# Order of low pieces, gate-up products and transposes in the expert stage of a retention-mLSTM block with expert-choice FFN

## Chip, cores and metric

The kernel runs on one core of one Trainium2 chip. The metric is the device time of one execution in microseconds (us); the median of several executions is compared. The engines are TensorE (PE, whose weight loads are shown apart as PEld), VectorE (DVE), ScalarE (ACT), GpSimd (POOL) and SyncE (SP, which here only issues loads).

## The reference, cut to what matters

One layer: `h = h + token_mixer(h)`, then `h = h + expert_choice_ffn(h)`, and a final norm. The change touches the second part. There are 528 tokens (16 of them meta tokens) of width 1024 and 16 experts; each expert takes the 66 tokens that score highest for it.

```
g, idx = lax.top_k(jnp.swapaxes(aff, 1, 2), cap)            # cap = 66
xs = jax.vmap(lambda ub, ib: ub[ib])(u, idx)                # [16, 66, 1024]
hid = (jax.nn.silu(jnp.einsum('becd,edf->becf', xs, w_gate))
       * jnp.einsum('becd,edf->becf', xs, w_up))            # [16, 66, 2816]
y = jnp.einsum('becf,efd->becd', hid, w_down) * g[..., None]
return jnp.zeros_like(h).at[jnp.arange(b_)[:, None, None], idx].add(y)
```

## The kernel before

All is float32 to the accuracy of three products: each operand is split into a high piece (rounded to fp32r by ACT, line 881) and a low piece (what is left, a subtraction on DVE, line 883), and each product is the sum of high x high (line 897), low input x high weight (898) and high input x low weight (899).

`experts` (line 840) runs 16 experts. Each has 48 slabs of weights, 128 x 1408 float32 (704 KB): gate half 0, up half 0, gate half 1, up half 1, with 8 slabs each (`wide`, 919), and down with 16 (`down`, 949; the last expert uses `last_down`, 963, with slabs of 1024 columns). `weights` (858) loads a slab through SP's queue into a ring of slabs. `product` (886) cuts a slab into two pieces of at most 768 columns, or into three of 512, 512 and 384 (the first slab of a projection, and some of down), splits each piece and issues the products on 66 rows. The pieces stand in two rings, six high and six low (three and three until the first expert's second half); that is three slabs.

Around the projections:

- `gate` (928): ACT writes the silu of the three gate banks into `hid` (line 931).
- `up` (933): DVE multiplies the three up banks into `hid` (line 937), in place.
- `hidden` (939): PE turns `hid` into 11 blocks of 128 x 66 (line 943, a transpose is a product with the identity), in two groups of 6 and 5; ACT and DVE split each group into `hT` (946, 947). It is called for half 0 after two slabs of gate half 1, and for half 1 after three slabs of down. Half 0 uses a `narrow` bank, half 1 a `wide` one.
- `gather` (902): POOL fetches the next expert's 66 rows by an indirect DMA (903), PE transposes them in two groups of four (910), DVE scales (915), ACT makes the high part of the input (916), POOL the low part (917).
- `scatter` (997): ACT weights the result (1000), POOL adds it to memory by an indirect DMA (1001).

The loop at line 1014 writes this order out. It is not the last word: the tile framework schedules each engine's instructions by a simulated timeline when the kernel is built, within the dependencies; each engine then executes its own list in order. `tc.issue_after(x)` adds an ordering edge: the instructions traced within it stand behind x on x's engine, with no semaphore. The generators (`wide`, `down`) yield after each slab, and `run(steps, n)` takes n slabs.

In names of the trace, left29t is the split input, right5t and left56t are the pieces, left24t is `hid` and left55t is `hT`; left25t to left48t are slabs.

Of the kernel before, what the change touches and what calls it, by code (L numbers as in the profile page):

```python
# [21 lines left out]
KT = 8  # L22
# [4 lines left out]
E = 16  # L27
CAP = 66
# [810 lines left out]
def experts(tc, a, bcast, left, right, routed, u_rows, h_rows, out):  # L839
# [5 lines left out]
    with ExitStack() as ctx:  # L845
# [31 lines left out]
        def split(src):  # L877
            n = src.shape[1]
            h = next(p_h)[:, :n]
            l = next(p_l)[:, :n]  # L880
            nc.scalar.activation(h, src, AF.Copy)  # L881
            with tc.issue_after(ready):
                nc.vector.tensor_sub(l, src, h)  # L883
            return h, l

        def product(slab, f0, cuts, target):
            n = slab.shape[1]
            for c0, c1 in zip((0,) + cuts, cuts + (n,)):
                h, l = split(slab[:, c0:c1])
                while c0 < c1:  # L890
# [8 lines left out]
                    nc.tensor.matmul(o, xh, l[:, w], start=False, stop=last)  # L899
                    c0 += m  # L900

        def gather(e):
# [4 lines left out]
            for g in range(2):  # L907
                b = bank()
                for j in range(4):
                    nc.tensor.transpose(b[:, j * CAP:(j + 1) * CAP], xg[:, 4 * g + j::KT], ident[:CAP, :CAP])  # L910
# [6 lines left out]
                (nc.gpsimd if e else nc.vector).tensor_sub(x_l[:, sl], v, x_h[:, sl])  # L917

# [9 lines left out]
        def gate(banks):  # L928
            for c, b in enumerate(banks):
                n = min(512, SLAB - 512 * c)  # L930
                nc.scalar.activation(hid[:CAP, 512 * c:512 * c + n], b[:CAP, :n], AF.Silu)

        def up(banks):
            for c, b in enumerate(banks):
                n = min(512, SLAB - 512 * c)
                s = slice(512 * c, 512 * c + n)
                nc.vector.tensor_mul(hid[:CAP, s], b[:CAP, :n], hid[:CAP, s])  # L937

        def hidden(hT, half):
            for f0, fn in ((0, 6), (6, 5)):  # L940
                b = bank("wide" if half else "narrow")
                for j in range(fn):
                    nc.tensor.transpose(b[:, j * CAP:(j + 1) * CAP], hid[:CAP, f0 + j:SLAB:RH], ident[:CAP, :CAP])  # L943
# [3 lines left out]
                nc.vector.tensor_sub(hT[:, 1, s], v, hT[:, 0, s])  # L947

# [61 lines left out]

        hT = None
        gather(0)
        nc.gpsimd.dma_start(tok, bass.AP(tensor=a["tok"].tensor, offset=a["tok"].offset, ap=[[0, CAP], [1, TOK]]))
        for e in range(E):
            g = wide(a["w_gate"], e, 0)
            gate(run(g))
            up(run(wide(a["w_up"], e, 0)))
            g = wide(a["w_gate"], e, 1)
            run(g, 2)
# [5 lines left out]
            hidden(hT, 0)  # L1025
            gate(run(g))
            up(run(wide(a["w_up"], e, 1)))
            if e == E - 1:
                break
            d = down(e, hT)  # L1030
            run(d, 3)
            hidden(hT, 1)
            gather(e + 1)
            scatter(e, run(d))
# [30 lines left out]
        d = last_down(E - 1, hT, 0)  # L1065
        run(d, 3)
        hidden(hT, 1)
        o = run(d)
# [73 lines left out]
```

## Time and profile before

| | us |
|---|---|
| median of 3 runs | 1989.85 (1989.01 to 1989.92) |
| profiled execution | 1988.62 |
| its span, first to last instruction | 1986.9 |
| granted clock of PE, mean over the span | 0.985 |

The expert stage runs from about 413 us to the end. Busy times are shares of the span. A row of a timeline has its start in us from the span's start, its length, engine, line and operation, output and inputs, the shapes, a count where rows are merged, and in brackets the idle time of the engine ahead of it with what ended that. Products overlap in the pipe, so the step from one start to the next, not the length, is what a product costs. A row of several instructions of one engine shows one length for all. A granted clock of 1.00 is 2.4 GHz, 0.50 is 1.2.

### The profile page before, as it was taken

How to read it: one execution, taken by the hardware profiler on the slowest of the kernel's cores; microseconds unless marked ns; L12 is line 12 of the kernel's file. 1: busy time of each engine (PE TensorE's matmuls, PEld its weight loads, DVE VectorE, ACT ScalarE, POOL GpSimd, SP SyncE). 2: the span in 40 equal slices, each digit the busy share in tenths (PEclk: the TensorE clock that was granted, in tenths of full speed). 3: DMA queues.
4: the chain of work that ended last, by engine and by line, in shares of the span. 5: the costliest groups of instructions: out<-in, count | busy, mean ns of one | idle time of the engine just before them, and what ended most of it. 6: DMA issues, size and time to landing. Idle time of an engine off the chain costs nothing.

```text
span 1986.9 us, 34790 instructions
## 1 busy us (share of the span) xinstructions
PE 1936.3 (97%) x12057; PEld 1513.4 (76%) x12057; DVE 1688.0 (85%) x2614; ACT 1450.9 (73%) x2417; POOL 307.4 (15%) x224
## 2 busy tenths in 40 slices
PE   8999999979999999999999999999999999999997
PEld 7989999767777777777777777777777777777674
DVE  7877776479999999898989888888888888888988
ACT  6565544277878888778777777787878787777776
POOL 1123221210000000030404010401030103030102
PEclk9999998989999999999999999999999999999999
DMA  4322214679999999999999999999999999999973
GB/s 156 98 77 76 65 56 169 233 283 361 373 362 378 352 392 350 363 368 360 376 357 377 352 370 352 382 354 363 360 363 365 353 366 362 371 367 368 344 280 115
DMA packets 134708, 604.60 MB, mean 304 GB/s; under 512 B 18597, under 2 KB 19237, under 8 KB 134531
## 3 DMA queue, kind: packets, MB, share of 16 engines
q1 hardware_dynamic: 123043, 565.28, 75.4%
q10 hardware_dynamic: 6656, 22.29, 3.3%
q0 software_dynamic: 4832, 14.82, 3.0%
q8 instruction: 94, 1.54, 0.3%
q14 instruction: 83, 0.68, 0.1%
HBM read 591.77 MB, written 10.55 MB: 303 GB/s over the span
## 4 chain that ended last, share of the span: by engine, by line
PE 90%; DVE 5%; DMA 2%; issue 1%; ACT 1%; POOL 0%; SPq 0%; POOLq 0%; DVEq 0%; ACTq 0%
PE wide L897 16%; PE wide L898 16%; PE wide L899 16%; PE narrow L899 8%; PE narrow L898 8%; PE narrow L897 8%; PE pj L210 2%; PE pj L211 2%; PE pj L212 2%; PE wide L943 1%; PE narrow L943 1%; DVE left24t L937 1%; PE pj L647 1%; PE pj L649 1%; PE pj L648 1%
## 5 line engine op out<-in xcount | busy, mean ns | idle before, releaser
L898 PE MATMUL wide<-right5t,left29t 128*66 128x512 f32 (+2 forms) x996 | 323.4, 329 | 0.5 <-DVE left29t L917 0.5
L897 PE MATMUL wide<-right5t,left29t 128*66 128x256 f32 (+2 forms) x996 | 316.7, 329 | 1.9 <-ACT left29t L916 1.6
L898 PE MATMUL wide<-left56t,left29t 128*66 128x256 f32 (+2 forms) x988 | 314.8, 326 | 0.0
L897 PE MATMUL wide<-left56t,left29t 128*66 128x256 f32 (+2 forms) x988 | 314.4, 327 | 0.0
L899 PE MATMUL wide<-right5t,left29t 128*66 128x512 f32 (+2 forms) x996 | 254.3, 330 | 0.3 <-DVE right5t L883 0.3
L899 PE MATMUL wide<-left56t,left29t 128*66 128x256 f32 (+2 forms) x988 | 245.4, 327 | 0.0
L897 PEld LDWEIGHTS wide<-left56t,left29t 128*66 128x66 f32 x988 | 135.0, 137 | 48.3 <-ACT left56t L881 1.7
L897 PEld LDWEIGHTS wide<-right5t,left29t 128*66 128x66 f32 x996 | 136.2, 137 | 43.0 <-ACT right5t L881 5.7
L899 PEld LDWEIGHTS wide<-right5t,left29t 128*66 128x66 f32 x996 | 134.6, 138 | 43.5 <-DVE right5t L883 0.7
L917 POOL TENSOR_TENSOR left29t<-right3t,left29t 128x264 fp32r<-128x264 f32 x30 | 155.7, 5206 | 70.6 <-ACT left29t L916 69.9
L899 PEld LDWEIGHTS wide<-left56t,left29t 128*66 128x66 f32 x988 | 132.3, 136 | 38.2
L903 POOL DMA_INDIRECT right3t<-u_rows,right3t x16 | 17.3, 1082 | 926.9 <-PE narrow L899 645.0
L898 PEld LDWEIGHTS wide<-left56t,left29t 128*66 128x66 f32 x988 | 134.5, 136 | 33.4
L898 PEld LDWEIGHTS wide<-right5t,left29t 128*66 128x66 f32 x996 | 136.1, 137 | 23.8 <-DVE left29t L917 0.9
L898 PE MATMUL narrow<-right5t,left55t 128*66 128x512 f32 x443 | 153.6, 352 | 0.0
L897 PE MATMUL narrow<-right5t,left55t 128*66 128x512 f32 x443 | 152.4, 352 | 0.0
L897 PE MATMUL narrow<-left56t,left55t 128*66 128x512 f32 (+1 forms) x441 | 151.4, 349 | 0.0
L210 PE MATMUL pj<-right1t,left2t 128*128 128x256 f32 (+1 forms) x496 | 144.5, 291 | 3.4 <-DVE left23t L387 3.4
L898 PE MATMUL narrow<-left56t,left55t 128*66 128x512 f32 (+1 forms) x441 | 147.6, 349 | 0.0
L211 PE MATMUL pj<-right2t,left2t 128*128 128x256 f32 (+1 forms) x496 | 143.6, 290 | 0.0
L212 PE MATMUL pj<-right1t,left3t 128*128 128x256 f32 (+1 forms) x496 | 143.2, 289 | 0.0
L899 PE MATMUL narrow<-right5t,left55t 128*66 128x512 f32 (+1 forms) x442 | 134.3, 355 | 0.7 <-DVE right5t L883 0.7
(497 smaller groups left out, 5057.6 us busy)
## 6 DMA issues: line engine op xcount, KB each, us to landing
left1t<-in_w_in_f ACTq DMA_DIRECT2D x30, 512.0 KB, 3.9
left43t<-in_w_up SPq DMA_DIRECT2D x12, 704.0 KB, 7.0
left42t<-in_w_up SPq DMA_DIRECT2D x12, 704.0 KB
left48t<-in_w_gate SPq DMA_DIRECT2D x12, 704.0 KB
left47t<-in_w_up SPq DMA_DIRECT2D x12, 704.0 KB, 6.3
left46t<-in_w_up SPq DMA_DIRECT2D x12, 704.0 KB
left25t<-in_w_up SPq DMA_DIRECT2D x12, 704.0 KB
left26t<-in_w_gate SPq DMA_DIRECT2D x12, 704.0 KB, 5.9
```

The source lines that it names most:

```text
L210: nc.tensor.matmul(ps[:, :ln], wh, x_h[:, k, l0:l0 + ln], start=(k == 0), stop=False)
L211: nc.tensor.matmul(ps[:, :ln], wh, x_l[:, k, l0:l0 + ln], start=False, stop=False)
L212: yield nc.tensor.matmul(ps[:, :ln], wl, x_h[:, k, l0:l0 + ln], start=False, stop=(k == KT - 1)).ins
L647: nc.tensor.matmul(ps[:, :ln], h, y_h[:, k, l0:l0 + ln], start=(j == 0), stop=False)
L648: nc.tensor.matmul(ps[:, :ln], h, y_l[:, k, l0:l0 + ln], start=False, stop=False)
L649: nc.tensor.matmul(ps[:, :ln], l, y_h[:, k, l0:l0 + ln], start=False, stop=(j == len(ks) - 1))
L897: nc.tensor.matmul(o, xh, h[:, w], start=start, stop=False)
L898: nc.tensor.matmul(o, xl, h[:, w], start=False, stop=False)
L899: nc.tensor.matmul(o, xh, l[:, w], start=False, stop=last)
L917: (nc.gpsimd if e else nc.vector).tensor_sub(x_l[:, sl], v, x_h[:, sl])
L937: nc.vector.tensor_mul(hid[:CAP, s], b[:CAP, :n], hid[:CAP, s])
L943: nc.tensor.transpose(b[:, j * CAP:(j + 1) * CAP], hid[:CAP, f0 + j:SLAB:RH], ident[:CAP, :CAP])
```

## The change

In each half of each expert the first slab of the next projection is traced ahead of `gate` and of `up`. In `up`, the first multiplication is put behind the last but one low piece traced so far, the other two behind the last one: these are the second and the third low piece of the next projection's first slab (in the last expert, whose down slabs have two pieces, the first and the second). `hidden` and `gather` become generators with one step per group of transposes. Each group of transposes is put behind the last product traced so far (`between`), and `paced` traces one slab behind each group. Half 0 starts after two slabs of gate half 1, half 1 after two of down (three before), and the gather's two groups follow those of half 1.

```diff
@@ split, product
-                nc.vector.tensor_sub(l, src, h)
+                lows.append(nc.vector.tensor_sub(l, src, h).ins)
             return h, l
+        latest = [None]
+        lows = []
...
-                    nc.tensor.matmul(o, xh, l[:, w], start=False, stop=last)
+                    latest[0] = nc.tensor.matmul(o, xh, l[:, w], start=False, stop=last).ins
                     c0 += m
+        def between():
+            return tc.issue_after(latest[0]) if latest[0] else nullcontext()
@@ gather (hidden in the same way)
-                for j in range(4):
-                    nc.tensor.transpose(b[:, j * CAP:(j + 1) * CAP], xg[:, 4 * g + j::KT], ident[:CAP, :CAP])
+                with between():
+                    for j in range(4):
+                        nc.tensor.transpose(b[:, j * CAP:(j + 1) * CAP], xg[:, 4 * g + j::KT], ident[:CAP, :CAP])
...
+                yield
@@ up
-                nc.vector.tensor_mul(hid[:CAP, s], b[:CAP, :n], hid[:CAP, s])
+                with tc.issue_after(lows[-1 if c else -2]):
+                    nc.vector.tensor_mul(hid[:CAP, s], b[:CAP, :n], hid[:CAP, s])
@@ the loop
+        def paced(steps, *others):
+            for x in others:
+                for _ in x:
+                    run(steps, 1)
+            return run(steps)
         hT = None
-        gather(0)
+        run(gather(0))
...
         for e in range(E):
-            g = wide(a["w_gate"], e, 0)
-            gate(run(g))
-            up(run(wide(a["w_up"], e, 0)))
+            g = run(wide(a["w_gate"], e, 0))
+            u = wide(a["w_up"], e, 0)
+            run(u, 1)
+            gate(g)
+            u = run(u)
             g = wide(a["w_gate"], e, 1)
-            run(g, 2)
+            run(g, 1)
+            up(u)
+            run(g, 1)
...
-            hidden(hT, 0)
-            gate(run(g))
-            up(run(wide(a["w_up"], e, 1)))
+            g = paced(g, hidden(hT, 0))
+            u = wide(a["w_up"], e, 1)
+            run(u, 1)
+            gate(g)
+            u = run(u)
+            d = last_down(E - 1, hT, 0) if e == E - 1 else down(e, hT)
+            run(d, 1)
+            up(u)
             if e == E - 1:
                 break
-            d = down(e, hT)
-            run(d, 3)
-            hidden(hT, 1)
-            gather(e + 1)
-            scatter(e, run(d))
+            run(d, 1)
+            scatter(e, paced(d, hidden(hT, 1), gather(e + 1)))
...
-        d = last_down(E - 1, hT, 0)
-        run(d, 3)
-        hidden(hT, 1)
-        o = run(d)
+        run(d, 1)
+        o = paced(d, hidden(hT, 1))
         d = last_down(E - 1, hT, 1)
```

## Rows read from the trace of the kernel before

**Rows 1.** The profile's page: the busy time of each engine in us with its share of the span and its instructions.

```profile
PE 1936.3 (97%) x12057; PEld 1513.4 (76%) x12057; DVE 1688.0 (85%) x2614; ACT 1450.9 (73%) x2417; POOL 307.4 (15%) x224
```

**Rows 2.** Busy time of each engine in two stretches of one expert each: start and end, length, then PE, PEld, DVE, ACT and POOL with their instructions, the granted clock, the DMA engines' busy share and GB/s.

```profile
591.50:686.90 95.40, 95.40 (x572) 71.71 (x571) 87.06 (x121) 78.93 (x122) 5.07 (x4) 1.00 0.99 369
971.00:1067.30 96.30, 96.03 (x572) 71.32 (x571) 84.98 (x121) 75.93 (x123) 21.59 (x5) 1.00 0.98 366
```

**Rows 3.** What SP's load queue waited for, the longest row: us in total, times, longest. left56t holds one part of the pieces, right5t the other.

```profile
SPq L866 <- DVE left56t L883: 613.2, 386, 14.2
```

**Rows 4.** Timeline of DVE around the multiplications of half 1 (line 937) in several experts. Between 965.55 and 966.76 stands one low piece of 512.

```profile
487.26 0.68 DVE L937 TENSOR_TENSOR left24t<-wide,left24t 66x512 f32<-66x512 f32 x1
...
772.74 0.83 DVE L883 TENSOR_TENSOR right5t<-left36t,right5t 128x640 fp32r<-128x640 f32 x1 [0.50 <-ACT right5t L881]
773.48 0.68 DVE L937 TENSOR_TENSOR left24t<-wide,left24t 66x512 f32<-66x512 f32 x1
...
869.18 0.69 DVE L937 TENSOR_TENSOR left24t<-wide,left24t 66x512 f32<-66x512 f32 x1 [1.84 <-PE wide L899]
...
965.55 0.69 DVE L937 TENSOR_TENSOR left24t<-wide,left24t 66x512 f32<-66x512 f32 x1 [1.85 <-PE wide L899]
966.76 1.15 DVE L937 TENSOR_TENSOR left24t<-wide,left24t 66x512 f32<-66x512 f32 x2
...
1158.22 0.69 DVE L937 TENSOR_TENSOR left24t<-wide,left24t 66x512 f32<-66x512 f32 x1 [1.85 <-PE wide L899]
...
1256.12 0.69 DVE L937 TENSOR_TENSOR left24t<-wide,left24t 66x512 f32<-66x512 f32 x1 [1.85 <-PE wide L899]
...
1935.25 1.75 DVE L937 TENSOR_TENSOR left24t<-wide,left24t 66x512 f32<-66x512 f32 x3 [0.53 <-PE wide L899]
```

**Rows 5.** Timeline of PE at the transposes of half 1 and of the gather in an early expert.

```profile
587.46 0.40 PE L898 MATMUL narrow<-left56t,left55t 128*66 128x512 f32 x1
587.69 1.44 PE L943 MATMUL wide<-right3t,left24t 66*128 66x66 f32 x11
588.96 0.27 PE L910 MATMUL wide<-right3t 66*128 66x66 f32 x1
589.04 0.54 PE L899 MATMUL narrow<-left56t,left55t 128*66 128x256 f32 x2
...
590.30 0.96 PE L910 MATMUL wide<-right3t 66*128 66x66 f32 x7
591.06 0.37 PE L897 MATMUL narrow<-right5t,left55t 128*66 128x384 f32 x1
```

**Rows 6.** The same for half 1 and the gather in a later expert.

```profile
1160.02 0.34 PE L898 MATMUL narrow<-right5t,left55t 128*66 128x384 f32 x1
1160.62 1.55 PE L943 MATMUL wide<-right3t,left24t 66*128 66x66 f32 x11 [0.27 <-DVE left24t L937]
1162.01 1.05 PE L910 MATMUL wide<-right3t 66*128 66x66 f32 x8
1162.87 0.46 PE L899 MATMUL narrow<-right5t,left55t 128*66 128x512 f32 x1
1163.13 0.62 PE L897 MATMUL narrow<-right5t,left55t 128*66 128x512 f32 x1
```

**Rows 7.** Stretches around the falls of the granted clock (PEclk), columns as in rows 2: ahead of the first fall within the expert stage's steady part, the first fall, and the last of four (the other two are at 1357 and 1552 us).

```profile
1159.70:1163.10 3.40, 3.13 (x24) 2.61 (x23) 3.40 (x6) 1.39 (x3) 0.00 (x0) 1.00 0.88 315
1163.10:1166.50 3.40, 3.40 (x13) 2.29 (x12) 3.40 (x8) 3.28 (x8) 3.06 (x2) 0.50 0.89 305
...
1842.40:1845.80 3.40, 3.40 (x13) 2.17 (x12) 3.40 (x7) 3.37 (x8) 2.24 (x1) 0.50 0.84 283
```

**Rows 8.** Timeline of ACT ahead of the mark at 965.55.

```profile
962.04 1.27 ACT L881 ACTIVATE right5t<-left47t 128x512 fp32r<-128x512 f32 x2 [0.39 <-PE wide L898]
```

**Rows 9.** Timeline of POOL in an early and in two later experts.

```profile
593.53 1.21 POOL L917 TENSOR_TENSOR left29t<-right3t,left29t 128x264 fp32r<-128x264 f32 x1 [0.58 <-ACT left29t L916]
...
875.38 19.15 POOL L917 TENSOR_TENSOR left29t<-right3t,left29t 128x264 fp32r<-128x264 f32 x2
...
1163.37 0.98 POOL L903 DMA_INDIRECT right3t<-u_rows,right3t  x1 [64.65 <-PE narrow L899]
```

**Rows 10.** Timeline of PE in the last expert: the transposes of half 1, and the waits in the tail.

```profile
1935.93 0.39 PE L898 MATMUL narrow<-right5t,left55t 128*66 128x512 f32 x1
1937.05 1.56 PE L943 MATMUL wide<-right3t,left24t 66*128 66x66 f32 x11 [0.73 <-DVE left24t L937]
...
1962.79 0.40 PE L898 MATMUL narrow<-left56t,left55t 128*66 128x512 f32 x1
1963.86 0.44 PE L899 MATMUL narrow<-right5t,left55t 128*66 128x512 f32 x1 [0.68 <-DVE right5t L883]
...
1968.47 0.45 PE L899 MATMUL narrow<-left56t,left55t 128*66 128x512 f32 x1 [0.69 <-DVE left56t L883]
```

**Rows 11.** Timeline of DVE behind the mark at 965.55.

```profile
968.89 0.81 DVE L883 TENSOR_TENSOR right5t<-left46t,right5t 128x640 fp32r<-128x640 f32 x1
969.62 0.95 DVE L883 TENSOR_TENSOR left56t<-left46t,left56t 128x768 fp32r<-128x768 f32 x1
```

**Rows 12.** Timeline of DVE around 890 us: a low piece of 384, and an idle time.

```profile
890.40 0.54 DVE L883 TENSOR_TENSOR right5t<-left25t,right5t 128x384 fp32r<-128x384 f32 x1
...
893.09 1.85 DVE L883 TENSOR_TENSOR right5t<-left26t,right5t 128x512 fp32r<-128x512 f32 x2 [0.35 <-ACT right5t L881]
```

More of the change, by code (lines that the diff above doesn't have):

```diff
@@ L1 @@
 import itertools
-from contextlib import ExitStack
+from contextlib import ExitStack, nullcontext
 import concourse.bass as bass
@@ L941, in hidden @@
                 b = bank("wide" if half else "narrow")
-                for j in range(fn):
-                    nc.tensor.transpose(b[:, j * CAP:(j + 1) * CAP], hid[:CAP, f0 + j:SLAB:RH], ident[:CAP, :CAP])
+                with between():
+                    for j in range(fn):
+                        nc.tensor.transpose(b[:, j * CAP:(j + 1) * CAP], hid[:CAP, f0 + j:SLAB:RH], ident[:CAP, :CAP])
                 v = b[:, :fn * CAP].rearrange("p (k c) -> p k c", c=CAP)
@@ L947, in hidden @@
                 nc.vector.tensor_sub(hT[:, 1, s], v, hT[:, 0, s])
+                yield
         def down(e, hT):
```

## The prediction

> **What bounds the kernel now.** I read the page first: TensorE (PE) is busy 97% of a span of 1986.9 us, VectorE (DVE) 85%, ScalarE (ACT) 73% [rows 1]. That alone says little, so next come the stretches of one expert each: PE is busy in 95.40 of 95.40 us in an early expert and in 96.03 of 96.30 us in a later one, with the DMA engines near 0.98 in both [rows 2]. The DMA share looks like a second bound. It is not one: the load queue waits 613.2 us for DVE to release slabs, on one part of the pieces alone [rows 3], so the loads run ahead and are held back. The expert stage is bound by PE, and only what makes PE wait or slows it can be won.
>
> The useful view is the period of the experts. The first multiplication of half 1 on DVE (line 937, first of three) reads the first bank that the up projection closes, so its start marks nearly the same place in every expert. I call it the mark. In the first experts the marks are at 487.26 and 773.48 us, three periods apart: 286.22 / 3 = 95.41 us. Then come 869.18 and 965.55 (96.37), 1158.22 and 1256.12 (97.90), and 1935.25 at the last expert [rows 4]. The same work thus has three periods, 95.41, 96.4 and 97.9, in one run.
>
> What differs is seen in two places. **Order on DVE.** In the early experts a low piece of the next projection's second slab (640 elements, line 883) already stands ahead of the mark and DVE hardly waits. In the later ones DVE sits idle for 1.85 us ahead of it, because the multiplications are queued in front of the first slab's low pieces [rows 4]. **Order on PE.** In the early form the 19 transposes behind half 1 stand as 12 and 7, products between, and the first follows its product of 512 columns after 0.23 us (587.46 to 587.69). In the later form they are one run, and PE goes from the product at 1160.02 to the transpose at 1160.62: 0.60 us where a product of 384 columns takes 0.23 x 384 / 512 = 0.17, so 0.43 us of waiting for DVE's multiplications [rows 5, 6]. In some periods the clock falls behind this run: granted 0.50 in the stretch from 1163.10 after one at 1.00, and so at four places, the last from 1842.40 [rows 7]. That is 1.2 GHz in place of 2.4.
>
> **The change part by part.**
>
> *Low pieces ahead of the multiplications.* At 32 places (two halves, 16 experts) the first multiplication goes behind two low pieces and the other two behind the third. No instruction is added. DVE's idle 1.85 us takes two pieces of 512 at 0.60 us (965.55 to 966.76 is one multiplication and one such piece) [rows 4], so they cost nothing, if their high pieces are there. ACT makes these, and its pieces of that slab (left47t) are done by 963.3, 2.2 us ahead of the mark [rows 8]. From the mark: first multiplication 0.60, third low piece 0.46 (0.54 less the 0.08 by which such rows overlap), the other two 1.07 (1.15 less 0.08), together 2.13 us. Now the later form takes 1.21 + 1.07 = 2.28 us [rows 4, 11, 12]. A small step earlier.
>
> *Transposes in groups.* In each half the first group waits for the last product of the second slab. A slab on PE takes (95.41 - 3.38) / 48 = 1.92 us, where 3.38 is the early transposes, 1.27 for each run of eleven, 0.08 and 0.76 [rows 5]. Two slabs are 3.83 us after the mark; the multiplications are done at 2.13. So the wait of PE for them, 0.43 us in each later expert, goes with 1.7 us to spare. It becomes no other wait that I can name: what is late next is the low pieces of the second slab (below). The transposes are as many as before. Six runs stand where the early form has three. The first product behind a run comes 0.26 after the one ahead of it rather than 0.23 (1162.87 to 1163.13, against 587.46 to 587.69) [rows 5, 6]: three more runs x 0.03 x 16 = 1.4 us. The ends: nothing, since seven transposes take 0.76 and eleven 1.27, no dearer each; and 0.12 a run, which is what a late run of eleven (1.39, 1160.62 to 1162.01) takes over an early one: 5.8 us. I take 1.4, nearest to the early rows.
>
> *Gather and hidden pieces as steps.* The gather's indirect DMA on POOL is traced one slab later, behind the two groups of hidden. It is issued at 1163.37, right behind the transposes of the gather before it (1162.01), and is wanted an expert later [rows 6, 9]; a step of 2 to 4 us is covered by some 90. The loads on SP keep their order; in the last expert one load of w_down now stands ahead of the four row loads, and SP's queue is held by slabs coming free anyway [rows 3]. The silu (ACT) is traced behind the first slab's high pieces; its result is used a projection (15 us) later. All of these: nothing, and if the slack were gone, one ACT step of 0.64 us (1.27 for two) per place [rows 8], inside the range's ends.
>
> *What the early order is worth.* The early experts already run with low pieces ahead and split transposes, without waits and at full clock. The change writes that order down for all. So I price it by the period: from 773.48 to 1935.25 are twelve periods, 1161.77 us, against 12 x 95.41 = 1144.92: 16.9 us [rows 4]. Of these the four falls of the clock are 4 x (97.90 - 96.37) = 6.1, the rest (10.8, 0.9 per expert) is the wait and the longer runs. Behind the last mark PE goes from 1935.93 to 1937.05, 1.12 where 0.23 is usual: 0.9 more [rows 10]. Sum: 16.9 + 0.9 - 1.4 = 16.4 us.
>
> Of the clock, [rows 7] show falls after a late run (0.43 us of waiting, 19 transposes); the early expert with the split form is at 1.00 throughout [rows 2]. The Trainium skill (TensorE: Matmul & The Clock Gate, "HAM oscillation") ties a falling clock to stretches in which PE sits idle. By that rule transposes are work, pacing them changes nothing about the falls, and the gain would be 10.3 us. The row speaks for the transposes: PE was busy 3.13 of 3.40 us ahead of the fall.
>
> **The sum.** The profiled execution took 1988.62 us, 1.72 outside its span; 1988.62 - 16.4 = 1972.2. The median of the runs is 1.23 above that execution: 1973.5 us, 0.8% faster. What measurement of this kernel can tell from no change is about 0.2%, 4 us.
>
> **The rivals.**
>
> 1. *The clock still falls.* Short runs of transposes may fall into the same stretch: against it, four early experts without one; for it, two groups of hidden and two of the gather come within 8 us. Four falls stay: 1973.5 + 6.1 = 1979.6.
>
> 2. *Low pieces of the second slab come late (slower).* After the mark DVE owes 2.13 us, then the second slab's pieces, 0.73 for 640 (968.89 to 969.62) and 0.87 for 768 (0.95 less 0.08) [rows 11]: 3.73 us. PE wants the last at about 3.83 - 0.29 = 3.54 (its product of 640 columns, 0.23 x 640 / 512), and the transposes that used to give DVE time now stand behind. Where PE has no high products to put in front, it waits, and the tail of the trace shows the price: 1.07 us from 1962.79 to 1963.86 where 0.23 is usual, so 0.84 us [rows 10]. Once at each of 32 places: 27 us, 1973.5 + 27 = 2000.4. It decides if the 0.2 us of lag is not covered. Against it: high products are put in front today (two products with high pieces stand ahead of the transposes of [rows 6], and the product with the low piece, line 899, comes behind), and there are pieces for three slabs.
>
> 3. *The gather's subtraction on POOL is locked out (slower).* One of its two instructions takes 1.21 us early, but both together 19.15 us later, ending where DVE sits idle for 0.35 us ahead of 893.09 [rows 9, 12]. The change fills DVE's idle time. If both groups waited 18 us, one after the other, from 10 us behind the mark, they would end 46 us behind it. The next projection starts at about 33 us (16 x 1.92 + 2.1 for transposes) and wants the second half of the low input four slabs later, at 41: 5 us x 15 = 75 us, 2048 us. The rule that says so is the Trainium skill's (SBUF — State Buffer, "SBUF: two separate sides"): DVE and GpSimd share ports under an exclusive lock, and the loser blocks; the rows agree. Against the price: DVE catches up sooner, since its 1.85 us are used, and the wait limits itself.
>
> 4. *The order does not change.* The pins might only restate what is scheduled in most places; then 1989.9. Against it: the late rows have the multiplications in front [rows 4].
>
> **How the numbers follow.** Forecast 0.78; rival 1, 0.08; rival 4, 0.05; rival 2, 0.06; rival 3, 0.03. Faster by over 0.2% is the forecast and rival 1: 0.86. Within: 0.05. Slower: 0.06 + 0.03 = 0.09. The range starts at 1989.9 - 17.8 (no cost for the runs) - 2.1, the three long waits of the tail (0.7 each, two of them shown) [rows 10] if DVE comes there with its lead, less 1 for the spread of runs: 1969. It ends at 1984: runs at 5.8 instead of 1.4 (1977.9) and the clock still falling (6.1).
>
> **What would show it.** Right: all marks some 95.4 to 95.5 us apart; low pieces ahead of each mark and no 1.85 us in front of it; no row of PE waiting on line 937; transposes in runs of 6, 5, 4, 4 with products between; a granted clock of 1.00 from 440 us to the tail. Wrong: waits of PE on line 883 outside the tail (rival 2), on the POOL subtraction (rival 3), half-rate stretches still there (rival 1), or periods of 96.4 still.

## The result, and the profile after

The changed kernel takes 1974.4 us (median, 1974.08 to 1977.21) beside 1989.43 us for the kernel before in the same runs: a ratio of 0.9929, 95% interval 0.9911 to 0.9946, so 0.7% faster. It ran a second time beside other kernels: 1976.22 against 1990.17, 0.9926, interval 0.9912 to 0.9939. The profiled execution took 1974.51 us with a span of 1972.8; the span of before was 1986.9. Forecast were 1973.5 us and a range of 1969 to 1984.

Line numbers moved with the edit: the products are lines 900 to 902 (897 to 899 before), the multiplications 947 (937), hidden's transposes 954 (943), the gather's 918 (910), its DMA 910 (903), its subtraction on POOL 925 (917), the silu 940. The pieces stay at 881 (high, ACT) and 883 (low, DVE).

The page first, against [rows 1]:

```profile
PE 1923.9 (98%) x12057; PEld 1511.5 (77%) x12057; DVE 1694.7 (86%) x2614; ACT 1455.4 (74%) x2417; POOL 177.6 (9%) x224
```

The instruction counts of PE and DVE are those of before. PE is busy 12.4 us less (1936.3 - 1923.9), out of 14.1 us of span. So most of what was won is PE doing the same instructions in less time, and some 1.7 us is idle time. The idle time understates the waits, though: of the 0.43 us that a step loses in [rows 6], the row has 0.27 as idle, and the rest counts as busy. POOL's busy time fell by 130 us, to which the last section comes back.

One early and one later expert, columns as in [rows 2]:

```profile
591.40:686.60 95.20, 95.20 (x572) 71.61 (x571) 87.22 (x121) 79.02 (x123) 4.80 (x4) 1.00 0.98 371
1064.00:1159.60 95.60, 95.60 (x572) 71.59 (x571) 85.82 (x121) 76.40 (x122) 3.93 (x4) 1.00 0.98 370
```

PE is busy in all of the later stretch too, at a granted clock of 1.00. In the whole expert stage of this trace, from 440 us to the tail, no stretch at 1.2 GHz is left; the next fall is at 1963.85, in the tail, where before had one as well.

The marks, on DVE, against [rows 4] (the first is early, the second the last one of the early form, the others late):

```profile
487.11 0.68 DVE L947 TENSOR_TENSOR left24t<-wide,left24t 66x512 f32<-66x512 f32 x1
...
772.85 0.68 DVE L947 TENSOR_TENSOR left24t<-wide,left24t 66x512 f32<-66x512 f32 x1
...
1057.72 0.69 DVE L883 TENSOR_TENSOR left56t<-left43t,left56t 128x512 fp32r<-128x512 f32 x1
1058.33 0.69 DVE L883 TENSOR_TENSOR right5t<-left43t,right5t 128x512 fp32r<-128x512 f32 x1
1059.66 0.69 DVE L947 TENSOR_TENSOR left24t<-wide,left24t 66x512 f32<-66x512 f32 x1 [0.65 <-PE wide L902]
1060.27 0.54 DVE L883 TENSOR_TENSOR right5t<-left43t,right5t 128x384 fp32r<-128x384 f32 x1
1060.73 1.14 DVE L947 TENSOR_TENSOR left24t<-wide,left24t 66x512 f32<-66x512 f32 x2
1061.80 0.81 DVE L883 TENSOR_TENSOR right5t<-left42t,right5t 128x640 fp32r<-128x640 f32 x1
...
1155.29 0.69 DVE L947 TENSOR_TENSOR left24t<-wide,left24t 66x512 f32<-66x512 f32 x1 [0.65 <-PE wide L902]
```

The order is the one the change writes down: two low pieces, the mark, the third low piece, the two other multiplications, the second slab. The multiplications end 2.14 us behind the mark, at the start of the next piece (1061.80 - 1059.66; forecast 2.13). DVE's idle time ahead of the mark went from 1.85 to 0.65, the 1.20 that two pieces of 512 take. The early period is (772.85 - 487.11) / 3 = 95.25 us, 0.16 less than before. The late one is 1155.29 - 1059.66 = 95.63, where before had 96.4 and, with a fall, 97.9.

PE at the same place, against [rows 6]:

```profile
1062.53 0.22 PE L901 MATMUL narrow<-right5t,left55t 128*66 128x128 f32 x1
1062.66 0.50 PE L902 MATMUL narrow<-right5t,left55t 128*66 128x128 f32 x2
...
1064.05 0.83 PE L954 MATMUL wide<-right3t,left24t 66*128 66x66 f32 x6
1064.69 0.31 PE L900 MATMUL narrow<-left56t,left55t 128*66 128x256 f32 x1
...
1066.63 0.77 PE L954 MATMUL wide<-right3t,left24t 66*128 66x66 f32 x5
...
1069.63 0.55 PE L918 MATMUL wide<-right3t 66*128 66x66 f32 x4
...
1071.96 0.55 PE L918 MATMUL wide<-right3t 66*128 66x66 f32 x4
```

Runs of 6, 5, 4 and 4, the first 4.39 us behind the mark, 2.25 us after the multiplications ended. No row of PE waits for line 947 in this trace. The only step at this place that is longer than a product is 1062.53 to 1062.66, 0.13 us where 128 columns take 0.06: the second slab's low piece of 640 (1061.80 on DVE, 0.81 long) is 0.07 us late.

**Where the 14.1 us came from.** The span divides at the marks: up to the fourth, 773.48 - 772.85 = 0.63; the twelve periods behind it, 1161.77 - (1920.65 - 772.85) = 13.97; the tail behind the last mark, 51.65 before and 52.15 after, -0.50. Sum 14.1.

One late period, taken apart by the steps of PE from one start to the next (each product at 0.23 us for 512 columns and in proportion, 91.08 us for 540 of them; what a step is longer than that counts as listed, and the last row holds all the excesses below 0.06 us):

| us in one late period | before (965.55) | after (1059.66) |
| --- | --- | --- |
| 540 products at their rate | 91.08 | 91.08 |
| 30 transposes | 3.62 | 3.08 |
| wait for the multiplications | 0.43 | 0 |
| wait for a low piece of the second slab | 0 | 0.07 |
| step at the scatter (first to second slab of the next gate) | 0.10 | 0.10 |
| small excesses | 1.10 | 1.30 |
| sum | 96.33 | 95.63 |

By this count the transposes gave more (0.54) than the wait (0.43 - 0.07 = 0.36), and the small excesses took 0.20 back. Apart from that, the twelve periods hold the four falls, 4 x 1.53 = 6.1 us.

### The profile page after: what moved, and what is told of

It reads as the page before. It is cut to its first block, busy times and chain, and to the rows that moved or that the text cites. A ratio compares the mean times of both kernels' runs of the same rounds, so it can differ in the third digit from the quotient of the medians.

```text
span 1972.8 us, 34817 instructions
## 1 busy us (share of the span) xinstructions
PE 1923.9 (98%) x12057; PEld 1511.5 (77%) x12057; DVE 1694.7 (86%) x2614; ACT 1455.4 (74%) x2417; POOL 177.6 (9%) x224
## 4 chain that ended last, share of the span: by engine, by line
PE 92%; DVE 4%; ACT 1%; DMA 1%; issue 1%; POOL 0%; POOLq 0%; SPq 0%; DVEq 0%; ACTq 0%
PE wide L900 16%; PE wide L902 16%; PE wide L901 16%; PE narrow L902 8%; PE narrow L901 8%; PE narrow L900 8%; PE pj L210 2%; PE pj L211 2%; PE pj L212 2%; PE wide L954 1%; PE narrow L954 1%; PE pj L647 1%; PE pj L649 1%; PE pj L648 1%; PE wide L918 1%
## 5 line engine op out<-in xcount | busy, mean ns | idle before, releaser
L900 PE MATMUL narrow<-left56t,left55t 128*66 128x512 f32 (+1 forms) x442 | 151.9, 347 | 0.0
L901 PE MATMUL narrow<-left56t,left55t 128*66 128x512 f32 (+1 forms) x442 | 146.1, 346 | 0.0
L902 PE MATMUL narrow<-left56t,left55t 128*66 128x512 f32 (+1 forms) x442 | 128.5, 346 | 1.8 <-DVE left56t L883 1.8
L210 PEld LDWEIGHTS pj<-right1t,left2t 128*128 128x128 f32 x496 | 96.2, 194 | 5.3 <-issue 2.9
```

What stands on the lines that cost most here:

```text
L210: nc.tensor.matmul(ps[:, :ln], wh, x_h[:, k, l0:l0 + ln], start=(k == 0), stop=False)
L900: nc.tensor.matmul(o, xh, h[:, w], start=start, stop=False)
L901: nc.tensor.matmul(o, xl, h[:, w], start=False, stop=False)
L902: latest[0] = nc.tensor.matmul(o, xh, l[:, w], start=False, stop=last).ins
```

## Experiments

All were timed in five rounds beside the kernel before. "Late period" is the distance of marks in the settled late experts of the profiled execution; "falls" are stretches at 1.2 GHz between 440 us and the tail.

| kernel | median us | ratio to before | late period | falls |
| --- | --- | --- | --- | --- |
| before | 1989.9 to 1990.5 | 1 | 96.37 (four of 97.9) | 4 |
| low pieces alone | 1989.93 | 1.0000 [0.9991, 1.0009] | 97.18 | 0 |
| pacing alone | 1999.50 | 1.0051 [1.0038, 1.0065] | 97.81 | 0 |
| changed, one run of transposes | 1976.50 | 0.9937 [0.9923, 0.9951] | 95.84 | 0 |
| low pieces alone, silu behind | 1977.67 | 0.9938 [0.9924, 0.9951] | 95.77 | 0 |
| before, gather apart | 1982.84 | 0.9962 [0.9949, 0.9976] | 96.37 | 0 |
| changed, silu in front | 2004.54 | 1.0068 [1.0054, 1.0082] | 98.4 (mean of nine) | 0 |
| changed, two slabs ahead | 1974.20 | 0.9927 [0.9914, 0.9941] | 95.47 | 0 |
| changed, scatter later | 1975.54 | 0.9926 [0.9912, 0.9939] | 95.63 | 0 |
| changed, both of these | 1976.71 | 0.9930 [0.9917, 0.9944] | 95.47 | 0 |
| changed, again | 1976.22 | 0.9926 [0.9912, 0.9939] | 95.63 | 0 |

**Low pieces alone.** The pins of the multiplications and the early tracing stay; the transposes are not paced.

```diff
-            return tc.issue_after(latest[0]) if latest[0] else nullcontext()
+            return nullcontext()
...
-            g = paced(g, hidden(hT, 0))
+            run(hidden(hT, 0))
+            g = run(g)
...
-            run(d, 1)
-            scatter(e, paced(d, hidden(hT, 1), gather(e + 1)))
+            run(d, 2)
+            run(hidden(hT, 1))
+            run(gather(e + 1))
+            scatter(e, run(d))
```

> Low pieces ahead of the multiplications, as in the change, but the transposes in one run each (11, and 19 behind half 1), without an ordering edge. Theory A (PE's wait for the multiplications and the long runs cost 0.9 us per later expert, and the falls of the clock need the wait): no row of PE waiting for a multiplication outside the last expert, marks 95.9 us apart (96.36 less the wait of 0.43), no fall of the clock, median about 1978. Theory B (a run of 19 transposes alone makes the clock fall): marks alternate between 95.9 and 97.4, some four falls stay, median about 1984. Theory C (only pacing counts, the order on DVE is idle): as the kernel before, 1989.

The time is theory C's, but not for its reason. The wait for the multiplications is gone outside the last expert and so are the falls, although the 19 transposes are one run again (eleven at 1065.57, eight at 1066.93): in this trace a run of 19 alone does not lower the clock, and the order on DVE does more than theory C allows. Yet nothing was won. PE of this kernel now waits at another place, the step from the gate to the up projection in half 0 (timeline of PE, and under it ACT):

```profile
1111.20 0.45 PE L902 MATMUL wide<-right5t,left29t 128*66 128x256 f32 x2
1112.21 0.45 PE L900 MATMUL wide<-right5t,left29t 128*66 128x512 f32 x1 [0.56 <-ACT right5t L881]
...
1114.74 0.45 PE L900 MATMUL wide<-left56t,left29t 128*66 128x512 f32 x1 [0.33 <-ACT left56t L881]
```

```profile
1111.05 0.60 ACT L940 ACTIVATE left24t<-wide 66x512 f32<-66x512 f32 x1 [4.30 <-PE wide L902]
1111.54 0.62 ACT L881 ACTIVATE right5t<-left41t 128x512 fp32r<-128x512 f32 x1
1112.06 1.03 ACT L881 ACTIVATE left56t<-left41t 128x512 fp32r<-128x512 f32 x2
1112.99 0.96 ACT L940 ACTIVATE left24t<-wide 66x512 f32<-66x512 f32 x2
```

ACT stood idle for 4.30 us, waiting for the first of the gate's three banks to close (in the gate's last slab) to read it with a silu, and the three high pieces of the first slab of the up projection were queued behind that silu. PE needs them the moment the gate is done. The two steps cost 0.72 and 0.49 us over a product, 1.21 per expert. The changed kernel has the high pieces first:

```profile
1103.61 0.62 ACT L881 ACTIVATE right5t<-left41t 128x512 fp32r<-128x512 f32 x1
1104.52 1.28 ACT L881 ACTIVATE left56t<-left41t 128x512 fp32r<-128x512 f32 x2 [0.30 <-PE wide L901]
1108.01 1.45 ACT L940 ACTIVATE left24t<-wide 66x512 f32<-66x512 f32 x3 [2.20 <-PE wide L902]
```

The program's text asks for the same order of silu and pieces in both kernels; it was the scheduling of instructions into ACT's queue that came out differently.

**Low pieces alone, silu behind.** To try that reading, the silus are held behind the last high piece of the first slab; nothing else differs from the kernel above.

```diff
-            nc.scalar.activation(h, src, AF.Copy)
+            highs.append(nc.scalar.activation(h, src, AF.Copy).ins)
...
-                nc.scalar.activation(hid[:CAP, 512 * c:512 * c + n], b[:CAP, :n], AF.Silu)
+                with tc.issue_after(highs[-1]):
+                    nc.scalar.activation(hid[:CAP, 512 * c:512 * c + n], b[:CAP, :n], AF.Silu)
```

> The low pieces ahead of the multiplications alone (no pacing, transposes of a half in one run), as in the first such kernel, but with the gate's silus put on ACT behind the last high piece of the next first slab, where the changed kernel has them. Theory A (the loss of the first such kernel is ACT's order alone: two waits of PE for high pieces, 0.72 + 0.49 = 1.21 us per expert): late periods 97.18 - 1.21, about 96.0 us, no wait of PE on ACT's high pieces there, no fall of the clock between 440 us and the tail, about 1989.9 - 12 x 1.2 = 1976 us, ratio about 0.993. Theory B (the loss belongs to the long, unpaced runs of transposes, which bring what comes next late whatever ACT's order is): periods stay near 97.2, about 1990 us, the wait going to another producer.

Theory A, more than in full: the period falls by 97.18 - 95.77 = 1.41 and the median by 12.3 us, with the long run kept (PE of this kernel):

```profile
1064.35 0.22 PE L902 MATMUL narrow<-right5t,left55t 128*66 128x128 f32 x1
1064.41 1.52 PE L956 MATMUL wide<-right3t,left24t 66*128 66x66 f32 x11
1065.77 1.05 PE L919 MATMUL wide<-right3t 66*128 66x66 f32 x8
```

The first transpose follows its product at once (1064.35, 128 columns, to 1064.41), with no pacing at all, so the written pacing is not needed for that. What covers the wait is PE's own queue. The multiplications end hardly earlier behind the mark than before (2.14 us against 2.28), but the first transpose stands 2.93 us behind it (1064.41 - 1061.48), where PE of before was ready for it at 1.97 (1160.02 + 0.17 - 1158.22): thirteen products of down stand ahead of the transposes now, seven before. With the low pieces there early, the scheduler put their products in front by itself. Measured by the period, this order of DVE, ACT and PE is worth 96.37 - 95.77 = 0.60 us per expert, and the pacing adds 0.14 (95.77 to 95.63).

**Changed kernel, silu in front.** The same place from the other side: in the changed kernel the gate's silus are traced ahead of the next slab again, and from the fifth expert on the three high pieces of half 0 are held behind the first silu, as in the first experiment.

```diff
-            g = run(wide(a["w_gate"], e, 0))
+            gate(run(wide(a["w_gate"], e, 0)))
+            held[:] = [silus[-3]] * 3 if e > 3 else []
...
-            gate(g)
...
-            nc.scalar.activation(h, src, AF.Copy)
+            with tc.issue_after(held.pop()) if held else nullcontext():
+                nc.scalar.activation(h, src, AF.Copy)
```

> The changed kernel with one thing undone: from the second half of the experts' early part on, the gate's first silu of half 0 stands on ACT ahead of the three high pieces of the next first slab. Low pieces, pins and paced transposes stay. Theory A (the silu's place is a part of the change with a price of its own: PE waits 0.72 + 0.49 = 1.21 us per expert for high pieces): late periods 95.63 + 1.21, about 96.8 us, no fall of the clock, about 1974.4 + 12 x 1.2 = 1989 us, ratio about 1.000. Theory B (the silu's place only mattered beside the long runs of transposes): periods 95.6 us, about 1974.5 us, ratio 0.993.

```profile
1116.71 0.59 ACT L943 ACTIVATE left24t<-wide 66x512 f32<-66x512 f32 x1 [4.14 <-PE wide L905]
1117.20 0.62 ACT L882 ACTIVATE right5t<-left41t 128x512 fp32r<-128x512 f32 x1
1117.72 1.03 ACT L882 ACTIVATE left56t<-left41t 128x512 fp32r<-128x512 f32 x2
```

```profile
1093.95 0.45 PE L903 MATMUL narrow<-left56t,left55t 128*66 128x512 f32 x1 [0.53 <-ACT left56t L882]
...
1117.87 0.45 PE L903 MATMUL wide<-right5t,left29t 128*66 128x512 f32 x1 [0.56 <-ACT right5t L882]
...
1120.39 0.46 PE L903 MATMUL wide<-left56t,left29t 128*66 128x512 f32 x1 [0.34 <-ACT left56t L882]
```

The two waits come back with the same lengths (steps 0.72 and 0.51 over a product): theory A's mechanism. Its time of 1989 us is 15 us too low, for the edit did more than it was meant to: pieces elsewhere were scheduled in another order as well and PE waits for some of them (0.53 at 1093.95), so the periods range from 94.3 to 101.5. The 1.2 us per expert is shown by both experiments; the rest of this kernel's loss is its own.

**Pacing alone.** The transposes are paced in groups; gate and up are traced as before and the pin on the low pieces is gone.

```diff
-                with tc.issue_after(lows[-1 if c else -2]):
-                    nc.vector.tensor_mul(hid[:CAP, s], b[:CAP, :n], hid[:CAP, s])
+                nc.vector.tensor_mul(hid[:CAP, s], b[:CAP, :n], hid[:CAP, s])
...
-            run(u, 1)
-            gate(g)
-            u = run(u)
...
-            up(u)
+            gate(g)
+            up(run(wide(a["w_up"], e, 1)))
```

> Transposes paced as in the change, but gate and up traced and queued as in the kernel before: the multiplications stand in front of the low pieces again. Theory A: the first group stands 3.8 us behind the mark and the multiplications end 2.28 us behind it, so pacing alone removes the wait and the falls: marks 95.6 to 95.8, DVE still idle 1.85 us ahead of each mark in the later experts, median 1974 to 1977. Rival (low pieces come late, 0.84 us a place): with the multiplications in front, the second slab's low pieces end at about 5 us behind the mark, PE waits on line 883 at most later places, marks 96 to 97, median 1980 to 1990. POOL's subtraction takes some 18 us again in the later experts and nobody waits for it.

Slower by half a per cent, and slower than either theory had it (1999.50 us; the rival's highest was 1990). DVE of this kernel idles ahead of the mark as before, and behind it the first slab's second piece comes only after the multiplications; PE (second fence) then waits for that piece instead:

```profile
1068.14 0.69 DVE L946 TENSOR_TENSOR left24t<-wide,left24t 66x512 f32<-66x512 f32 x1 [1.85 <-PE wide L902]
...
1069.35 1.15 DVE L946 TENSOR_TENSOR left24t<-wide,left24t 66x512 f32<-66x512 f32 x2
1070.41 1.15 DVE L883 TENSOR_TENSOR right5t<-left43t,right5t 128x512 fp32r<-128x512 f32 x2
```

```profile
1069.94 0.34 PE L901 MATMUL narrow<-right5t,left55t 128*66 128x384 f32 x1
1071.15 0.44 PE L902 MATMUL narrow<-right5t,left55t 128*66 128x512 f32 x1 [0.87 <-DVE right5t L883]
```

This is the wait of the prediction's rival 2, at the first slab instead of the second and with its cover removed: the transposes used to give DVE time for the low pieces, and moved back they leave PE 1.04 us short (1.21 less 0.17) at half 1, and 0.6 and 0.3 us at half 0. The text of the expectation also had POOL's subtraction at some 18 us again; each of its two instructions took some 0.77. Of the two parts of the change, then, low pieces alone give nothing as ACT's queue was scheduled there, and pacing alone costs.

**Changed kernel, one run of transposes.** Pins and the edge to the second slab stay; the groups of one place follow one another.

```diff
             for x in others:
-                for _ in x:
-                    run(steps, 1)
+                run(x)
```

> The change with its edges, but all transposes of a place in one run behind the second slab: 11 behind half 0, 19 behind half 1 and the gather. Theory A: no wait, since the edge holds them behind the multiplications, so no fall of the clock; longer runs cost what the rows show (3.38 or 3.62 us of transposes per expert against 3.08 in the short runs of the changed kernel): marks 95.9 to 96.1, median 1978 to 1982. Theory B (the run of 19 alone makes the clock fall): four falls or more of 1.5 us on top, median 1984 to 1989.

The period is 95.84, 0.21 above that of the changed kernel and just under theory A's 95.9, and there is no fall: the grouping is worth 0.2 us per expert, some 2.5 us in all, and the clock does not depend on it. The times (0.9937 and 0.9929; 1976.50 us where theory A had 1978 at the least) can't tell the two apart; the periods of the traces do.

**Before, gather apart.** In the kernel before, the gather's eight transposes are traced one slab behind hidden's eleven and held there on PE by an ordering edge. The multiplications stay in front, and with them PE's wait.

```diff
-                for j in range(4):
-                    nc.tensor.transpose(b[:, j * CAP:(j + 1) * CAP], xg[:, 4 * g + j::KT], ident[:CAP, :CAP])
+                with tc.issue_after(latest[0]) if latest[0] else ExitStack():
+                    for j in range(4):
+                        nc.tensor.transpose(b[:, j * CAP:(j + 1) * CAP], xg[:, 4 * g + j::KT], ident[:CAP, :CAP])
...
             hidden(hT, 1)
+            run(d, 1)
             gather(e + 1)
```

> The kernel before with one edit: the gather's eight transposes stand one slab behind hidden's eleven, and the multiplications stay in front of the low pieces, so the 0.43 us wait of PE stays too. Theory A (the clock falls where the wait and a run of 19 transposes come together): no fall between 440 us and the tail, late periods all about 96.3 us, four falls x 1.53 = 6.1 us less, about 1983.5 us, ratio 0.997. Theory B (the wait is enough for a fall, whatever the length of the run): falls stay, about 1989.5 us, ratio 1.000.

Theory A holds, in size too: 7.3 us faster by the medians (forecast 6), all late periods 96.37, and no fall with the wait still there (timeline of PE, then a window around the place of the last of [rows 7], columns as in rows 2):

```profile
1060.59 0.34 PE L899 MATMUL narrow<-right5t,left55t 128*66 128x384 f32 x1
1061.20 1.55 PE L945 MATMUL wide<-right3t,left24t 66*128 66x66 f32 x11 [0.27 <-DVE left24t L939]
...
1069.28 0.99 PE L912 MATMUL wide<-right3t 66*128 66x66 f32 x8
```

```profile
1842.00:1846.00 4.00, 4.00 (x25) 2.78 (x24) 4.00 (x7) 3.28 (x7) 3.76 (x1) 1.00 0.89 341
```

The eight transposes come 6.7 us of products behind the eleven. The wait without the run of 19 makes no fall, and the run without the wait makes none either (the three kernels above that keep it). Before has both at eleven places, and falls at four of them; in its last expert, with a wait of 0.73 us and a run of 11 alone, it does not fall. The other executions of both kernels agree with the traced ones: the granted clock, as a mean over the span, is 0.988 to 0.991 in the five of this kernel and 0.985 to 0.987 in the nine of before beside it. What decides at which four is not settled.

**What is left: low pieces and scatter.** Three variants of the changed kernel went after the 0.38 us by which its late period exceeds its early one. Two slabs of low pieces ahead of the multiplications:

```diff
-            run(g, 1)
+            run(g, 2)
             up(u)
...
-            run(d, 1)
+            run(d, 2)
             up(u)
```

> The changed kernel with two slabs of low pieces, not one, ahead of the multiplications of up, and the transposes behind the third. Theory A (what is left of the late excess, 0.13 us per period, and the 1.14 us step in the last expert are low pieces of the second slab that come late): periods about 95.5 us, the step in the last expert gone, 13 x 0.13 + 0.9 = 2.6 us less, about 1972 us. Theory B (the slack is used up: the multiplications, now about 1.5 us later, come late for the transposes or the third slab's low pieces come late instead): periods 95.6 us or more, 1974.4 us or more, with the wait at another place.

The late low-piece wait is gone and the period is 95.47, 0.16 less, as theory A has it. The step in the last expert is not gone (1923.71 to 1924.85, 1.14 us): it waits for a low piece one slab later, still behind the last two multiplications, as theory B has it. The span of the profiled execution is 1.4 us below that of the changed kernel; the medians do not tell them apart. The scatter's step was to go by tracing the next gate's first slab ahead of the scatter:

```diff
-            g = run(wide(a["w_gate"], e, 0))
+            g = run(wide(a["w_gate"], e, 0) if e == 0 else nxt)
...
-            scatter(e, paced(d, hidden(hT, 1), gather(e + 1)))
+            o = paced(d, hidden(hT, 1), gather(e + 1))
+            nxt = wide(a["w_gate"], e + 1, 0)
+            run(nxt, 1)
+            scatter(e, o)
```

> The change, and two steps more: the next expert's first gate slab is traced ahead of scatter, and in the last expert two slabs of down stand ahead of the multiplications. If what is left of the later periods (95.63 against 95.25) is ACT's weighting of the result in front of the first slab's high pieces (0.15 us at each of 12 places) and the wait of 0.91 us in the last expert is DVE's order there, the marks come 95.45 to 95.5 apart, the last wait goes, median 1971 to 1972.5. If the 0.15 us only moves on, and the last wait only moves to the multiplications: 1974.4.

The period is 95.63 and the 0.10 us step is still there, at the same place: 35.03 us behind the mark in both kernels (1094.69 - 1059.66 and 1095.69 - 1060.66). Nor did it move, for the edit changed nothing on ACT. In both kernels the weighting stands behind the first gate slab's high pieces and ahead of the second's (the changed kernel, then this one):

```profile
1092.92 1.26 ACT L1012 ACTIVATE left30t<-narrow,right3t 66x512 f32<-66x512 f32 x2 [1.55 <-PE narrow L902]
1094.07 1.46 ACT L881 ACTIVATE right5t<-left48t 128x768 fp32r<-128x768 f32 x2
```

```profile
1093.92 1.26 ACT L1012 ACTIVATE left30t<-narrow,right3t 66x512 f32<-66x512 f32 x2 [1.55 <-PE narrow L902]
1095.08 1.46 ACT L881 ACTIVATE right5t<-left48t 128x768 fp32r<-128x768 f32 x2
```

The edit restates an order that the scheduler had already chosen, so what the scatter costs is not tested. For that reading speaks an early expert of the changed kernel, where the weighting stands behind the high pieces of the second and the third slab and PE has no such step:

```profile
711.56 0.73 ACT L881 ACTIVATE left56t<-left41t 128x640 fp32r<-128x640 f32 x1
712.18 1.24 ACT L1012 ACTIVATE left30t<-narrow,right3t 66x512 f32<-66x512 f32 x2
```

(This kernel also had the second slab of low pieces in the last expert; its step of 1.14 us stayed, at 1925.03.) Both edits together:

> The changed kernel with two slabs of low pieces ahead of the multiplications and the next gate's first slab ahead of the scatter. Theory A (both leftovers of the late period are of one kind, and their gains add): periods 95.63 - 0.16 - 0.10, about 95.4 us, tail 50 us or less, about 1972 us, ratio 0.991 to 0.992. Theory B (the scatter's 0.10 us is only moved, as before): periods 95.47 us, about 1974 us, ratio 0.9927.

95.47, the two-slab gain alone: theory B's number, but the scatter's place on ACT did not change here either. The changed kernel ran along for comparison:

> The changed kernel once more, beside the others on the same chip. All theories: about 1974.4 us, ratio 0.992 to 0.993, periods 95.63 us, no fall of the clock between 440 us and the tail.

It gave 1976.22 us and the same periods to a few hundredths. No variant beats the changed kernel by more than the measurement can tell.

## Why the prediction was right, and where its terms were off

**The order on DVE** came as worked out, 2.14 us against 2.13 behind the mark, and the pieces ahead of the mark cost nothing. The forecast's mechanism holds: with the low pieces in front and the transposes 4.39 us behind the mark, PE does not wait for the multiplications.

**That the wait goes because of the second slab** was only half the reason. The prediction gave the pacing 3.83 us of room; without pacing (silu behind) the wait is gone as well, because the scheduler puts the low pieces' products ahead of the transposes, 2.93 us behind the mark. What the second slab's edge does is use room that the low pieces had made; without them it makes PE wait for those pieces (pacing alone).

**The silu** was priced at nothing, with 0.64 us of ACT a place as the bound if its slack were gone. The cover was named wrongly. The result of the silu is wanted a projection later; but a silu that stands ahead of the next high pieces waits 4.1 to 4.3 us for the first of the gate's banks to close, and those pieces, queued behind it on ACT, are wanted at once. Behind the pieces it costs nothing, ahead of them 1.21 us per expert. In the kernel before, this wait is not there, so the change could not win by it; but where ACT's order is lost, the low pieces win nothing (low pieces alone). That the changed kernel kept the good order is the scheduler's doing, and the forecast was lucky there. The step that failed is the question what is queued behind a waiting instruction, not asked for ACT.

**The transposes** were charged 1.4 us for three more runs per expert. The sign was wrong. Short runs are cheaper: the 30 transposes of one expert take 3.08 us in runs of 6, 5, 4, 4 and 6, 5 where the early form of before took 3.37 and the late one 3.62. A run of six moves on after 0.64 us, 0.107 each, against 0.126 in a run of eleven (1160.62 to 1162.01, [rows 6]). The products around the runs give 0.13 of that back (small excesses 0.96 before and 1.09 after, both early). Net, the early period is 0.16 shorter. The prediction read one step behind a run, 0.03 us longer, and did not weigh the run itself.

**The periods** were to be 95.4 to 95.5 and are 95.63. Of the 0.38 above the early 95.25, 0.07 is the low piece of the second slab, so rival 2 came true at less than a tenth of its price of 0.84; 0.10 is the step at the scatter (read from the rows, not tested); 0.21 is spread over products in steps too small to name, 0.09 of it gone with two slabs of low pieces ahead (1.30 to 1.21). What makes the rest is open.

**The last expert** was to give 0.9 us and gave nothing: its wait passed from the multiplications to a low piece, against [rows 10].

```profile
1922.50 0.40 PE L901 MATMUL narrow<-left56t,left55t 128*66 128x512 f32 x1
1923.64 0.45 PE L902 MATMUL narrow<-right5t,left55t 128*66 128x512 f32 x1 [0.75 <-DVE right5t L883]
```

```profile
1920.65 0.68 DVE L947 TENSOR_TENSOR left24t<-wide,left24t 66x512 f32<-66x512 f32 x1
...
1921.85 1.14 DVE L947 TENSOR_TENSOR left24t<-wide,left24t 66x512 f32<-66x512 f32 x2
1922.91 1.28 DVE L883 TENSOR_TENSOR right5t<-left45t,left56t 128x512 fp32r<-128x512 f32 x2
```

In this projection a slab has two pieces of 512 columns, with three products and some 0.7 us of PE each, while DVE still owes two multiplications (1921.85, 1.14 us) ahead of the second slab's low pieces (1922.91). PE is there 0.9 us early. That is rival 2, near its full price, at the one place where its lag is not covered. The tail's three long waits (0.70 to 0.72 us on line 883) also stayed.

**The clock.** The four falls went, 6.1 us as forecast, but the prediction had only half of the cause. It set the long run of transposes against idle time, the cause in the Trainium skill's rule (TensorE: Matmul & The Clock Gate, "HAM oscillation"), and took the side of the run. The traces show a fall only with both: none with the wait and runs of 11 and 8, none with the run of 19 and no wait. That transposes are work by that rule was the prediction's own addition; the section speaks of idle time alone. It also drew the consequence wrongly: were the 0.43 us of idle time the cause, low pieces ahead would take it away as well, the falls would go, and the 10.3 us given for it should have been the same 16.4. And the idle stretches of that section are a kernel's waits for DMA between its tiles, far longer than 0.43 us, so the rule as it stands there accounts for no fall here. The same page ("A second HAM failure mode: psum-queue depth-cycling") tells of a clock that swings with frequent short idle times between groups of matmuls; the trace agrees only in so far as the idle time ahead of a fall was as short as 0.43 us; it is one wait in an expert, not a frequent one.

**The sum.** Forecast 16.4 us, measured 14.1 in the profiled executions: falls 6.1 as forecast; the rest of the twelve periods, with the transposes' term in it, 7.9 against 10.8 - 1.4 = 9.4; the early periods 0.6 (not forecast); last expert and tail -0.5 against +0.9. That the median came within 0.9 us of the forecast is in part luck: by the medians the gain is 15.0 us, and errors of both signs (transposes and early periods better, late periods and last expert worse) cancel in it.

## What to carry to other kernels

When an early part of a loop runs at a shorter period than the later part with the same work, the early order is the target, and the difference of the periods is the prize; then ask on every engine, not only on the two that meet in the wait, what is queued behind an instruction that waits. An order pinned on one engine is worth what the other queues' order lets through: here the low pieces without ACT's order gave nothing, the pacing without the low pieces cost 0.5%, the low pieces with ACT's order gave 0.6% and all three 0.7%, two that only the periods tell apart (95.77 and 95.63 us).

## What the hardware showed that was not expected

**The shared port has two losers.** The prediction feared that POOL's subtraction would wait for DVE (19.15 us for both in [rows 9]). In the changed kernel it is DVE that waits (timelines of POOL and DVE):

```profile
1073.82 1.47 POOL L925 TENSOR_TENSOR left29t<-right3t,left29t 128x264 fp32r<-128x264 f32 x2
```

```profile
1073.70 2.61 DVE L883 TENSOR_TENSOR left56t<-left40t,left56t 128x384 fp32r<-128x384 f32 x2
```

The two subtractions take 0.76 and 0.75 us, and the DVE piece beside them, of 384 columns, lasts 2.01 us instead of 0.54: longer by 1.47, the time of both. In the kernel with the gather apart POOL loses again, 11.4 us for the first subtraction, which ends right behind DVE's next gap (0.34 us ahead of 1082.71). The Trainium skill (SBUF — State Buffer, "SBUF: two separate sides") says that whichever starts first gets the pair of ports and the other waits. That one of the two waits for all of the other's time agrees; who started first the rows do not settle, since DVE's piece starts on record at 1073.70, 0.12 us ahead of POOL's, and is the one that waits. DVE's 1.47 us per expert delayed no product here.

**Neither the wait nor the long run alone lowered the clock**, in four traces with one of the two (one with the wait, three with the run) beside the trace of before, which has both at eleven places and falls at four.
